# State-space heads of a hybrid block: the weighting, the inter-chunk output and the state update written with other instructions on other engines

## The chip, the cores and the metric

One core of a Trainium2 chip runs the whole kernel. The metric is the device time of one execution in microseconds; lower is better. The engines are TensorE (PE), VectorE (DVE), ScalarE (ACT), GpSimd (POOL) and SyncE (SP, which issues DMAs). Each takes its instructions from a queue of its own, in order.

## The reference

Two layers of a diffusion transformer block over 512 latent and 256 context tokens of 1024 features. Each layer projects the normalized tokens once and gives the columns to three kinds of heads: 6 of softmax attention, 4 of retention, 6 of a bidirectional state-space recurrence (SSD); an output projection and a squared-ReLU MLP follow. The recurrence in chunks of 128 tokens, cut to what matters here:

```python
scores = jnp.einsum('bhcin,bhcjn->bhcij', qc, kc) * decay
y_intra = jnp.einsum('bhcij,bhcjp->bhcip', scores, vc)
d_state = jnp.einsum('bhcj,bhcjn,bhcjp->bhcnp', jnp.exp(last - cum), kc, vc)
chunk_decay = jnp.exp(last[..., 0])
def step(s, inp):
    dec, ds = inp
    return dec[..., None, None] * s + ds, s
...
y_inter = jnp.exp(cum)[..., None] * jnp.einsum('bhcin,bhcnp->bhcip', qc, s_in)
return (y_intra + y_inter).reshape(b, h, l, p), s_final
```

It is run once forward and once backward; the keys of each direction are weighted by that direction's step size (dt), and the two outputs are added.

## The kernel before

Weights come from HBM and are split into a high and a low part, so that each product is three matmuls (`mm3`). Tokens lie in 6 tiles of 128: four latent, two context. In layer 0 the queries of all tiles are wanted (NQ = 6), in layer 1 only the latent ones (NQ = 4).

The state-space stage of a layer runs at about 148 to 262 us (layer 0) and 1219 to 1312 us (layer 1). Its loop goes over the heads h = 0 to 5 and mixes three things into each turn.

*Filling matmuls.* `run(fill, 1)` issues one tile of the query projection (24 matmuls `qap`), later of the gate z (`zp`). For each qap tile ACT copies the result out, POOL multiplies the gain (L570) and rotates it (L554 to L557).

*Inside a chunk* (`ssd_head_a`, `ssd_head_b`). Two matmuls broadcast the cumulative decays over the partitions (F, L747 and L749); ACT (L752), DVE (L754) and ACT again make the decay matrix `a`. The weighted scores `tb` join two triangles of `gfb` (the products of C and B, masked), one scaled by the forward step size, the other by the backward one: POOL writes the second for all tiles (L757), DVE adds the first, tile by tile, as scalar_tensor_tensor, STT (L759), and POOL multiplies by `a` (L760). PE then multiplies tb by the inputs (`yi`, L769), and DVE adds the result to `y_tok` (L771).

*Between chunks* (`ssd_state(i)`, one step of both directions). DVE weights the inputs (`vw`, L784). From the second step on PE multiplies the state `S` by C (`in`, L788), and DVE scales the result by the decay `expf` of the token and adds it to y_tok, head by head (L792). PE makes the step's state (`ds`, L797), and DVE scales S by the chunk's decay and adds ds, head by head (L803).

Behind the loop POOL multiplies y_tok by the gate (L869), ACT sums the squares and DVE makes the root from `ssq` (L871). Then attention starts: scores `s` (L938), the row maximum on DVE (L940, L943), probabilities `P` (L944, L949) and their transposes `pt`. The maximum needs `qrs`, the root of the queries' sums of squares, in three iterations of L165 to L167.

The program states dependences only: a scheduler fixes each engine's order when the kernel is built, within the limits of the pools. The matmul results `yi`, `in` and `ds` share one PSUM pool (pC) of two buffers, taken in turn; `s1` (vw, rotation scratch) has 3 buffers, `t3` (a, tb) 4, `u3` 6.

Of the kernel before, what the change touches and what calls it, by code (L numbers as in the profile page):

```python
# [14 lines left out]
AF = mybir.ActivationFunctionType  # L15
ALU = mybir.AluOpType
AX = mybir.AxisListType
PSUM = bass.MemoryType.PSUM
DRAM = bass.MemoryType.DRAM

D = 1024
# [13 lines left out]
# columns of w_in  # L35
QA, KA, VA, QR, KR, VR, GR, Z0, XBC, DT0 = 0, 384, 512, 640, 896, 1152, 1408, 1664, 2048, 2944
# rows of the per-layer parameters that are used as columns
R_B, R_G, R_CW, R_CB, R_SG, R_END = 0, 48, 80, 115, 122, 125
# columns of the per-layer parameters that are used on every partition
# [3 lines left out]
def shape_constants():  # L43
# [16 lines left out]
    # query minus key in a chunk; steps from the chunk before to a query, for both directions  # L60
# [20 lines left out]
def tile_hybrid_backbone(  # L81
# [87 lines left out]
    def rsqrt_mean(y, ssum, use, D=D, n=1):  # L169
        """1 / sqrt(ssum / D + EPS): the scalar engine's root, then one Newton step on its reciprocal"""  # L170
# [12 lines left out]
    def softplus(y, xin, n):  # L183
        """log(1 + exp(x)) = max(x, 0) + 2 atanh(e / (2 + e)), e = exp(-|x|)"""
# [17 lines left out]
    def wraw(src, shape, name):  # L202
        """one half of a unit: at most 1024 elements a partition"""
# [6 lines left out]
    def wunit(src, shape, name, lo_eng=None, pool=None):  # L210
        """src: function (first row block, row blocks) -> list of (AP, first column, columns)"""
# [13 lines left out]
    def wcols(w, k0, cols):  # L225
        """row blocks from k0 on; cols: list of (column in w, column in the unit, columns)"""
        return lambda a0, an: [(krows(w, k0 + a0, an, c, n), o, n) for c, o, n in cols]
# [21 lines left out]
    # gate * norm gain: [mixer or channel, stream]  # L249
    grow = [dp.tile([2, 2, D], F32, name=f"grow{l}") for l in range(DEPTH)]  # L250
    pcol = [cp.tile([128, R_END], F32, name=f"pcol{l}") for l in range(DEPTH)]
    # per layer: A1, B1, A2, B2, each [chunk, stream]
# [18 lines left out]
    def mod_cols(l, sec, q, nrow):  # L271
        """section of 512 columns of the modulation, as per-feature columns; q: [nrow, 512] in SBUF"""
# [75 lines left out]
    def mod_sums(l, sec, acc, raw=None):  # L348
        """the same, with the sums over the chunks off the tensor engine; acc [128, 2, 512]"""
# [22 lines left out]
    def cond_cols(n):  # L372
        """silu of both conditionings: [partition, chunk of 128 / n features, stream], the same on n groups of partitions"""
# [15 lines left out]
    def mod_groups(secs, acc, cs):  # L389
        """sections [(layer, section)] side by side on groups of partitions; acc [128, 2, 512]"""  # L390
# [27 lines left out]
    def gate_row(pool, l, which, stream):  # L418
        """(gate * norm_g) of one stream on every partition; which 0: mixer, 1: channel"""
# [1054 lines left out]
```

## Time and profile before

| | |
|---|---|
| runs (three) | 1886.2, 1888.09 (median), 1888.5 us |
| span of the profiled execution | 1880.8 us |
| busy: PE, DVE, ACT, POOL | 93%, 65%, 37%, 20% |
| mean granted TensorE clock | 0.972 |
| bytes moved | 217 MB, 115 GB/s over the span |

A run's time is taken around the whole launch, the span runs from the first to the last instruction of the one execution that was profiled; the median lies 7.3 us above it. The shares of busy time are averages over stages that differ, so the stage that is changed has to be read by itself, from the waits of the engine that is busiest in it.

### The profile page before, as it was taken

How to read it: one execution, taken by the hardware profiler on the slowest of the kernel's cores; microseconds unless marked ns; L12 is line 12 of the kernel's file. 1: busy time of each engine (PE TensorE's matmuls, PEld its weight loads, DVE VectorE, ACT ScalarE, POOL GpSimd, SP SyncE). 2: the span in 40 equal slices, each digit the busy share in tenths (PEclk: the TensorE clock that was granted, in tenths of full speed). 3: DMA queues.
4: the chain of work that ended last, by engine and by line, in shares of the span. 5: the costliest groups of instructions: out<-in, count | busy, mean ns of one | idle time of the engine just before them, and what ended most of it. 6: DMA issues, size and time to landing. Idle time of an engine off the chain costs nothing. (4 is left out here: it accounts for less than half of the span.)

```text
span 1880.8 us, 24641 instructions
## 1 busy us (share of the span) xinstructions
PE 1753.1 (93%) x8991; PEld 1443.0 (77%) x8991; DVE 1219.7 (65%) x2462; ACT 703.0 (37%) x1267; POOL 369.1 (20%) x391
## 2 busy tenths in 40 slices
PE   6987999997999999999999979888987999999998
PEld 2877977655878888888888868777866788888886
DVE  5868985664668566566566586788876654444445
ACT  5543376652461111201201275433772532222222
POOL 0047232313001100100100132553022021111112
PEclk9999999997999999999999999999996999999999
DMA  8410243366444334434434433224324432222332
GB/s 274 124 52 32 89 149 104 104 182 184 146 135 136 124 101 132 125 107 123 126 105 118 152 123 91 65 71 124 100 73 110 147 122 90 90 90 91 102 105 95
DMA packets 189078, 217.00 MB, mean 115 GB/s; under 512 B 67667, under 2 KB 142237, under 8 KB 188957
## 3 DMA queue, kind: packets, MB, share of 16 engines
q1 hardware_dynamic: 188956, 215.43, 37.8%
q8 instruction: 71, 1.16, 0.2%
q14 instruction: 51, 0.41, 0.1%
HBM read 189.66 MB, written 25.72 MB: 115 GB/s over the span
## 5 line engine op out<-in xcount | busy, mean ns | idle before, releaser
L467 PE MATMUL f<-h_h,wh_f 128*128 128x512 f32 (+1 forms) x800 | 280.3, 351 | 1.4 <-ACT h_h L448 1.4
L469 PE MATMUL f<-h_h,wl_f 128*128 128x512 f32 (+1 forms) x800 | 281.0, 352 | 0.0
L468 PE MATMUL f<-h_l,wh_f 128*128 128x512 f32 (+1 forms) x800 | 280.1, 350 | 0.8 <-DVE h_l L449 0.8
L1299 POOL TENSOR_TENSOR r<-r 128x768 f32<-128x768 f32 (+1 forms) x64 | 93.8, 1466 | 847.4 <-ACT r L1298 837.8
L467 PE MATMUL f<-wh_g,uh 128*128 128x512 f32 x640 | 253.0, 396 | 4.1 <-DVE acc L1327 1.7
L468 PE MATMUL f<-wl_g,uh 128*128 128x512 f32 x640 | 252.6, 395 | 0.0
L469 PE MATMUL f<-wh_g,ul 128*128 128x512 f32 x640 | 251.8, 394 | 0.0
L221 ACT ACTIVATE wh_f<-wr_f 128x1024 fp32r<-128x1024 f32 x64 | 66.5, 1055 | 377.2 <-PE f L469 164.4
L1329 DVE TENSOR_TENSOR acc<-acc,f 128x512 f32<-128x512 f32 x140 | 96.0, 686 | 121.0 <-PE f L469 119.6
L467 PEld LDWEIGHTS f<-h_h,wh_f 128*128 128x128 f32 x800 | 152.0, 190 | 23.0 <-ACT h_h L448 1.5
L468 PEld LDWEIGHTS f<-h_l,wh_f 128*128 128x128 f32 x800 | 151.1, 189 | 22.8 <-DVE h_l L449 1.0
L469 PEld LDWEIGHTS f<-h_h,wl_f 128*128 128x128 f32 x800 | 151.2, 189 | 20.8
L405 DVE SCALAR_TENSOR_TENSOR ga<-wr_mg,cg_a,ga 128x512 f32<-128x512 f32 x216 | 153.6, 762 | 14.6 <-DMA wr_mg<-in_w_mod_dram 14.6
L467 PEld LDWEIGHTS f<-wh_g,uh 128*128 128x128 f32 x640 | 120.1, 188 | 33.5 <-DVE acc L1327 2.2
L469 PEld LDWEIGHTS f<-wh_g,ul 128*128 128x128 f32 x640 | 120.1, 188 | 28.8
L468 PEld LDWEIGHTS f<-wl_g,uh 128*128 128x128 f32 x640 | 120.2, 188 | 27.4 <-DVE wl_g L222 0.2
L1298 ACT ACTIVATE r<-f 128x768 f32<-128x768 f32 (+1 forms) x64 | 44.8, 699 | 193.4 <-PE f L469 133.4
L1300 DVE CAST uh<-r 128x768 fp32r<-128x768 f32 (+1 forms) x64 | 32.3, 505 | 123.2 <-POOL r L1299 123.2
L222 DVE TENSOR_TENSOR wl_f<-wr_f,wh_f 128x1024 fp32r<-128x1024 f32 x64 | 77.6, 1220 | 51.3 <-ACT wh_f L221 51.3
L222 DVE TENSOR_TENSOR wl_g<-wr_g,wh_g 128x1024 fp32r<-128x1024 f32 x62 | 76.6, 1241 | 50.9 <-ACT wh_g L221 50.8
L221 ACT ACTIVATE wh_g<-wr_g 128x1024 fp32r<-128x1024 f32 x64 | 67.3, 1056 | 94.2 <-DMA wr_g<-in_w_ff_dram 53.6
L467 PE MATMUL xbc<-h_h,wh_xbc 128*128 128x512 f32 (+1 forms) x208 | 73.5, 353 | 7.7 <-ACT cin L692 7.7
(405 smaller groups left out, 3774.3 us busy)
## 6 DMA issues: line engine op xcount, KB each, us to landing
wr_f<-in_w_ff_dram SPq DMA_DIRECT2D x64, 512.0 KB, 3.7
wr_g<-in_w_ff_dram SPq DMA_DIRECT2D x64, 512.0 KB, 3.5
wr_mg<-in_w_mod_dram SPq DMA_DIRECT2D x192, 128.0 KB, 2.9
wr_m<-in_w_mod_dram SPq DMA_DIRECT2D x24, 512.0 KB, 3.8
m<-in_w_mod_dram SPq DMA_DIRECT2D x32, 256.0 KB, 4.2
wr_o<-in_w_out_dram SPq DMA_DIRECT2D x16, 512.0 KB, 4.1
wr_xbc<-in_w_in_dram SPq DMA_DIRECT2D x14, 512.0 KB, 5.3
xmid<-xt SPq DMA_DIRECT2D x10, 512.0 KB, 2.6
```

The lines of the kernel that those rows point to most:

```text
L221: S.activation(hv[:, a0 : a0 + an], r, AF.Copy)
L222: (lo_eng or V).tensor_tensor(lv[:, a0 : a0 + an], r, hv[:, a0 : a0 + an].bitcast(F32), ALU.subtract)
L405: V.scalar_tensor_tensor(acc[:, s], r2[:, k % 2], w, acc[:, s], ALU.mult, ALU.add)
L467: T.matmul(o, a[0], b[0], start=first, stop=False)
L468: T.matmul(o, a[0], b[1], start=False, stop=False)
L469: T.matmul(o, a[1], b[0], start=False, stop=last)
L1298: S.activation(r, q[:, :NT], AF.Relu)
L1299: G.tensor_tensor(r, r, r, ALU.mult)
L1300: V.tensor_copy(uh, r)
L1329: V.tensor_tensor(acc[tt][:, ns], acc[tt][:, ns], qs[tt][half], ALU.add)
```

## The change

Three places, all in the state-space stage. The weighted scores: POOL writes its triangle into a tile of its own, `tw` (pool u3); ACT writes the scaled other triangle into tb, tile by tile; one DVE addition joins them. The inter-chunk output: one DVE multiplication over all six heads writes `ys` (pool s1), and POOL adds it to y_tok. The state: POOL scales S for all six heads, and one DVE addition adds ds. Comments and docstrings are gone as well, so lines behind the first place are numbered one, later two and then one higher; the new lines are L758 (tw), L760 (ACT), L761 (DVE), L762 (POOL, tb by a), L794 (ys), L795 (POOL, y_tok), L804 (POOL, S), L805 (DVE, S), and vw is L786, in L790, ds L799, yi L771.

```diff
             tb = t3([128, 6, 128], f"tb{h}")
-            G.tensor_tensor(tb[:, :NQ], gf[:, 1, :NQ], bc(dtv[:, :NQ, 6 + h], 2, 128), ALU.mult)
+            tw = u3([128, 6, 128], f"tw{h}")
+            G.tensor_tensor(tw[:, :NQ], gf[:, 1, :NQ], bc(dtv[:, :NQ, 6 + h], 2, 128), ALU.mult)
             for t in range(NQ):
-                V.scalar_tensor_tensor(tb[:, t, :], gf[:, 0, t, :], dtv[:, t, h : h + 1], tb[:, t, :], ALU.mult, ALU.add)
+                S.activation(tb[:, t, :], gf[:, 0, t, :], AF.Copy, scale=dtv[:, t, h : h + 1])
+            V.tensor_tensor(tb[:, :NQ], tb[:, :NQ], tw[:, :NQ], ALU.add)
             G.tensor_tensor(tb[:, :NQ], tb[:, :NQ], a[:, :NQ], ALU.mult)
             mats[h] = tb
...
                     yv = v3(y_tok[:, t])
-                    for h in range(6):
-                        V.scalar_tensor_tensor(yv[:, h, :], q[:, h, :], expf[:, t, 6 * d + h : 6 * d + h + 1], yv[:, h, :],
-                                               ALU.mult, ALU.add)
+                    ys = s1([128, 6, 64], "ys")
+                    V.tensor_tensor(ys, q, bc(expf[:, t, hs], 2, 64), ALU.mult)
+                    G.tensor_tensor(yv, yv, ys, ALU.add)
...
                     if i == 0:
                         S.activation(st, q, AF.Copy)
                     else:
-                        for h in range(6):
-                            V.scalar_tensor_tensor(st[:, h, :], st[:, h, :], dec[:, t, 6 * d + h : 6 * d + h + 1], q[:, h, :],
-                                                   ALU.mult, ALU.add)
+                        G.tensor_tensor(st, st, bc(dec[:, t, hs], 2, 64), ALU.mult)
+                        V.tensor_tensor(st, st, q, ALU.add)
```

The scheduler's orders differ at many places; three of them follow. The first is POOL's queue in layer 0, from the first triangle of tb to the second tb product. Before (a number behind a name tells buffers apart: tb_1371 and tw_1372 are head 0's, tb_1467 or tb_1469 head 1's, st_qa_1566 or st_qa_1570 the query tile 2):

```order
L757 TENSOR_TENSOR tb_1371<-gfb_1348,dtv_664 128x768
L757 TENSOR_TENSOR tb_1467<-gfb_1348,dtv_664 128x768
L760 TENSOR_TENSOR tb_1371<-tb_1371,a_1351 128x768
L570 TENSOR_TENSOR st_qa_1566<-st_qa_1566,par_479 128x384
L554 TENSOR_TENSOR rp_1572<-st_qa_1566,cst_486 128x12x16
L555 TENSOR_TENSOR rp_1572<-st_qa_1566,cst_486 128x12x16
L556 TENSOR_TENSOR st_qa_1566<-st_qa_1566,cst_486 128x384
L557 TENSOR_TENSOR st_qa_1566<-st_qa_1566,rp_1572 128x384
L757 TENSOR_TENSOR tb_1598<-gfb_1348,dtv_664 128x768
L760 TENSOR_TENSOR tb_1467<-tb_1467,a_1447 128x768
```

After:

```order
L758 TENSOR_TENSOR tw_1372<-gfb_1348,dtv_664 128x768
L758 TENSOR_TENSOR tw_1470<-gfb_1348,dtv_664 128x768
L758 TENSOR_TENSOR tw_1603<-gfb_1348,dtv_664 128x768
L762 TENSOR_TENSOR tb_1371<-tb_1371,a_1351 128x768
L758 TENSOR_TENSOR tw_1739<-gfb_1389,dtv_664 128x768
L570 TENSOR_TENSOR st_qa_1570<-st_qa_1570,par_479 128x384
L554 TENSOR_TENSOR rp_1576<-st_qa_1570,cst_486 128x12x16
L555 TENSOR_TENSOR rp_1576<-st_qa_1570,cst_486 128x12x16
L556 TENSOR_TENSOR st_qa_1570<-st_qa_1570,cst_486 128x384
L758 TENSOR_TENSOR tw_1889<-gfb_1389,dtv_664 128x768
L762 TENSOR_TENSOR tb_1469<-tb_1469,a_1449 128x768
```

Three tw stand ahead of the first tb product instead of two first halves of tb, and two more between it and the second one. The queue goes on after that with the state of both directions (S_1336 forward, S_1337 backward) and the next query tile:

```order
L557 TENSOR_TENSOR st_qa_1570<-st_qa_1570,rp_1576 128x384
L804 TENSOR_TENSOR S_1336<-S_1336,dec_668 128x384
L570 TENSOR_TENSOR st_qa_1638<-st_qa_1638,par_479 128x384
L554 TENSOR_TENSOR rp_1644<-st_qa_1638,cst_486 128x12x16
L555 TENSOR_TENSOR rp_1644<-st_qa_1638,cst_486 128x12x16
L762 TENSOR_TENSOR tb_1602<-tb_1602,a_1582 128x768
L556 TENSOR_TENSOR st_qa_1638<-st_qa_1638,cst_486 128x384
L758 TENSOR_TENSOR tw_2018<-gfb_1389,dtv_664 128x768
L557 TENSOR_TENSOR st_qa_1638<-st_qa_1638,rp_1644 128x384
L795 TENSOR_TENSOR y_tok_1335<-y_tok_1335,ys_1655 128x384
L804 TENSOR_TENSOR S_1337<-S_1337,dec_668 128x384
L795 TENSOR_TENSOR y_tok_1335<-y_tok_1335,ys_1668 128x384
```

The backward state's L804 stands behind a rotation, head 2's tb product, a tw and a y_tok addition; before, POOL had nothing to do with S.

The second place is PE's queue in layer 0, in the second step (i = 1) and up to head 1's yi. Before, from the backward `in` on:

```order
L788 MATMUL in_1666<-S_1337,CT_978 128x192
L788 MATMUL in_1666<-S_1337,CT_1098 128x192
L749 MATMUL F_1736<-frow_671,onehot 128x256
L467 MATMUL qap_1755<-wh_qa_1390,h_h 128x384
L468 MATMUL qap_1755<-wl_qa_1391,h_h 128x384
L469 MATMUL qap_1755<-wh_qa_1390,h_l 128x384
L467 MATMUL qap_1755<-wh_qa_1390,h_h 128x384
L468 MATMUL qap_1755<-wl_qa_1391,h_h 128x384
L469 MATMUL qap_1755<-wh_qa_1390,h_l 128x384
L467 MATMUL qap_1755<-wh_qa_1390,h_h 128x384
L797 MATMUL ds_1675<-vw_1664,b_tok_673 128x192 x2
```

After, from the same `in` (in_1665) to yi of head 1 (yi_1676 and yi_1682, where yi_1684 was before):

```order
L790 MATMUL in_1665<-S_1337,CT_978 128x192
L790 MATMUL in_1665<-S_1337,CT_1098 128x192
L469 MATMUL qap_1686<-wh_qa_1392,h_l 128x384
L467 MATMUL qap_1686<-wh_qa_1402,h_h 128x384
L468 MATMUL qap_1686<-wl_qa_1403,h_h 128x384
L469 MATMUL qap_1686<-wh_qa_1402,h_l 128x384
L799 MATMUL ds_1671<-vw_1663,b_tok_673 128x192 x2
L771 MATMUL yi_1676<-xs_tok_672,tb_1469 128x128 x4
L771 MATMUL yi_1682<-xs_tok_672,tb_1469 128x128 x2
L467 MATMUL qap_1686<-wh_qa_1402,h_h 128x384
L468 MATMUL qap_1686<-wl_qa_1403,h_h 128x384
L469 MATMUL qap_1686<-wh_qa_1402,h_l 128x384
```

In the new order the two yi stand behind four qap matmuls and ds; before, twelve qap matmuls and ds lay between `in` and the first yi (the last five of the twelve are not shown), and four more between the two.

The third place is DVE's queue in layer 1, where the roots qrs are made. Before, its last iterations, among the start of attention:

```order
L165 TENSOR_TENSOR rq_t<-qrs_10548 128x36
L900 TENSOR_TENSOR qla_11350<-dTqa_11344,qha_11349 128x512
L166 TENSOR_TENSOR rq_t<-rq_t,rq_h 128x36
L940 TENSOR_REDUCE mx_11354<-s_11357 128x1
L167 SCALAR_TENSOR_TENSOR qrs_10548<-rq_t,qrs_10548 128x36
L940 TENSOR_REDUCE mx_11354<-s_11380 128x1
L165 TENSOR_TENSOR rq_t<-qrs_10548 128x36
L222 TENSOR_TENSOR wl_qg_12080<-wr_qg_0_12081,wh_qg_12079 128x1024
L871 TENSOR_SCALAR ssq_11216<-ssq_11216 128x6
L166 TENSOR_TENSOR rq_t<-rq_t,rq_h 128x36
L222 TENSOR_TENSOR wl_qg_12080<-wr_qg_2_12086,wh_qg_12079 128x1024
L158 TENSOR_SCALAR rq_t<-ssq_11216 128x6
```

After, right behind the fourth head's first instructions, where tb_10860 is head 3's:

```order
L159 TENSOR_SCALAR qrs_10498<-rq_t 128x36
L842 SCALAR_TENSOR_TENSOR st_zt_10840<-st_zt_10840,zh_10841 128x384
L754 SCALAR_TENSOR_TENSOR a_10846<-F_10853,ncol_9893,a_10846 128x128 x4
L165 TENSOR_TENSOR rq_t<-qrs_10498 128x36
L166 TENSOR_TENSOR rq_t<-rq_t,rq_h 128x36
L167 SCALAR_TENSOR_TENSOR qrs_10498<-rq_t,qrs_10498 128x36
L761 TENSOR_TENSOR tb_10860<-tb_10860,tw_10861 128x512
L165 TENSOR_TENSOR rq_t<-qrs_10498 128x36
L166 TENSOR_TENSOR rq_t<-rq_t,rq_h 128x36
L167 SCALAR_TENSOR_TENSOR qrs_10498<-rq_t,qrs_10498 128x36
L165 TENSOR_TENSOR rq_t<-qrs_10498 128x36
L166 TENSOR_TENSOR rq_t<-rq_t,rq_h 128x36
```

All three iterations stand ahead of the third step's vw now, and wl_qg's two halves (L222) stand in the fifth step, ahead of L941. In front of the first row maximum stands ssq instead:

```order
L910 TENSOR_TENSOR vat_11163<-vraw_11161,vat_11163 128x12x64
L893 SCALAR_TENSOR_TENSOR k1a_11232<-dTka_11225,k1a_11232 64x768
L901 TENSOR_TENSOR qla_11244<-dTqa_11238,qha_11243 128x512
L901 TENSOR_TENSOR qla_11256<-dTqa_11250,qha_11255 128x512
L872 TENSOR_SCALAR ssq_11122<-ssq_11122 128x6
L941 TENSOR_REDUCE mx_11260<-s_11263 128x1
L158 TENSOR_SCALAR rq_t<-ssq_11122 128x6
L160 TENSOR_SCALAR rq_h<-ssq_11122 128x6
L944 TENSOR_TENSOR mx_11260<-mx_11260,qrs_10498 128x1
```

## Rows read from the trace of the kernel before

**Rows 1.** The page: busy time of each engine, share of the span, instructions.

```profile
PE 1753.1 (93%) x8991; PEld 1443.0 (77%) x8991; DVE 1219.7 (65%) x2462; ACT 703.0 (37%) x1267; POOL 369.1 (20%) x391
```

**Rows 2.** PE's waits in layer 0, 148 to 262 us: total, times, longest.

```profile
PE ds L797 <- DVE vw L784: 4.4, 2, 2.7
PE yi L769 <- POOL tb L760: 3.6, 1, 3.6
PE s L938 <- DVE rq_t L165: 1.7, 1, 1.7
PE in L788 <- DVE y_tok L771: 1.6, 1, 1.6
...
PE in L788 <- DVE y_tok L792: 1.1, 1, 1.1
```

**Rows 3.** PE's waits in layer 1, 1219 to 1315 us, same columns.

```profile
PE ds L797 <- DVE vw L784: 5.9, 4, 2.5
PE yi L769 <- POOL tb L760: 3.7, 1, 3.7
PE s L938 <- ACT P L944: 2.3, 1, 2.3
...
PE pt L152 <- DVE P L949: 1.1, 1, 1.1
PE s L938 <- DVE qla L900: 0.8, 1, 0.8
```

**Rows 4.** Windows of layer 0: us, busy of each engine, granted clock, DMA share, GB/s.

```profile
core 0: us, PE busy (x) PEld busy (x) DVE busy (x) ACT busy (x) POOL busy (x), PEclk, DMA share, GB/s
...
160.00:170.00 10.00, 6.99 (x35) 6.85 (x36) 10.00 (x20) 2.39 (x7) 7.80 (x8) 0.83 0.06 20
```

**Rows 5.** Windows of layer 1 where attention begins, same columns.

```profile
1300.00:1310.00 10.00, 6.67 (x27) 4.90 (x26) 9.68 (x24) 3.25 (x8) 8.78 (x12) 0.86 0.40 118
1310.00:1330.00 20.00, 20.00 (x110) 16.74 (x111) 14.03 (x33) 15.46 (x32) 2.35 (x4) 0.90 0.29 82
```

**Rows 6.** Lines 759, 792 and 803: duration ns min/median/max, first and last start, forms.

```profile
L759 DVE SCALAR_TENSOR_TENSOR tb<-gfb,dtv,tb x60: 332/342/1566, 158.1 to 1282.3; 128x128 f32<-128x128 f32 x60
...
L792 DVE SCALAR_TENSOR_TENSOR y_tok<-in,expf,y_tok x108: 265/273/285, 179.9 to 1293.6; 128x64 f32<-128x64 f32 x108
...
L803 DVE SCALAR_TENSOR_TENSOR S<-S,dec,ds x96: 264/275/282, 181.0 to 1289.0; 128x64 f32<-128x64 f32 x96
```

**Rows 7.** Prices: three lines as in rows 6, and ACT's timeline at 157 us.

```profile
L222 DVE TENSOR_TENSOR wl_z<-wr_z,wh_z x8: 948/958/1352, 137.3 to 1245.1; 128x768 fp32r<-128x768 f32 x8
...
L784 DVE TENSOR_TENSOR vw<-xs_tok,wst x20: 544/551/2014, 150.0 to 1285.8; 128x384 f32<-128x384 f32 x20
...
L570 POOL TENSOR_TENSOR st_qa<-st_qa,par x10: 991/1016/1310, 142.7 to 1243.5; 128x384 f32<-128x384 f32 x10
...
157.08 1.66 ACT L752 ACTIVATE a<-F,ncol 128x128 f32<-128x128 f32 x6 [0.37 <-PE F L749]
```

**Rows 8.** Timeline at 178 us: start, us, engine, line, operation; idle before, releaser.

```profile
177.98 1.97 DVE L784 TENSOR_TENSOR vw<-xs_tok,wst 128x384 f32<-128x384 f32 x1
...
177.74 1.80 POOL L760 TENSOR_TENSOR tb<-tb,a 128x768 f32<-128x768 f32 x1 [1.35 <-DVE tb L759]
```

**Rows 9.** POOL's timeline in layer 0.

```profile
156.60 2.92 POOL L757 TENSOR_TENSOR tb<-gfb,dtv 128x768 f32<-128x768 f32 x2
161.15 1.80 POOL L760 TENSOR_TENSOR tb<-tb,a 128x768 f32<-128x768 f32 x1 [1.63 <-DVE tb L759]
...
164.04 0.60 POOL L554 TENSOR_TENSOR rp<-st_qa,cst 128x192 f32<-128x192 f32 x1
...
166.36 1.01 POOL L557 TENSOR_TENSOR st_qa<-st_qa,rp 128x384 f32<-128x384 f32 x1
```

**Rows 10.** POOL's timeline in layer 1.

```profile
1226.44 2.05 POOL L757 TENSOR_TENSOR tb<-gfb,dtv 128x512 f32<-128x512 f32 x2
1229.59 1.26 POOL L760 TENSOR_TENSOR tb<-tb,a 128x512 f32<-128x512 f32 x1 [1.10 <-DVE tb L759]
```

## The prediction

> **What bounds the kernel now.** I began with the busy shares of the page [rows 1]: PE works 93% of the span, the other engines 65%, 37% and 20%. So the time changes only where PE stands still or runs slowly, and an instruction saved on DVE is worth nothing unless PE waits for it. The change lies in two short stretches, the state-space stages of the two layers, and the second view is what PE waits for there. In layer 0 [rows 2] the six longest stalls are 2.7 + 1.7 (the rest of the 4.4) for DVE's vw, 3.6 for POOL's tb, 1.6 and 1.1 for DVE's y_tok, and 1.7 for DVE's rq_t where attention begins: 12.4 us. In layer 1 [rows 3] they are 5.9 for vw in four pieces, 3.7 for tb, and 0.8, 2.3 and 1.1 at the start of attention: 13.8 us.
>
> The third view gives what a stall costs on top. In windows of 10 us the granted clock is 0.83 right behind the 3.6 us stall of layer 0 [rows 4], and the same in three other windows of the two stages: behind the 2.7 us stall (180 to 190), and in layer 1 behind 3.7 us (1230 to 1240) and 2.5 us (1240 to 1250). A mean of 0.83 between the levels 1.0 and 0.5 is 10 x 0.17 / 0.5 = 3.4 us at the lower one, half of it lost: 1.7 us. The windows behind the shorter stalls, 1.7 us and less, show 1.00, so I count 1.7 us for each stall of 2.5 us or more. The start of attention in layer 1 [rows 5] has 0.86 and then 0.90 over 20 us: 1.4 + 2.0 = 3.4 us. **Ledger before:** layer 0 12.4 + 2 x 1.7 = 15.8 us; layer 1 13.8 + 2 x 1.7 + 3.4 = 20.6 us.
>
> **What the change takes from DVE.** Medians are 342, 273 and 275 ns [rows 6]. Layer 0 has 36 + 60 + 48 of them: 12.3 + 16.4 + 13.2 = 41.9 us. Layer 1 has 24 + 48 + 48: 34.5 us. What comes instead: one tb addition a head (priced by the 128x768 subtraction of two SBUF tiles, 0.95 us [rows 7]; two thirds of it, 0.64, for layer 1's 512 columns) and, for each step and direction, one ys and (from the second step) one S addition at 0.55 us, the price of vw, which has the same 128x384 [rows 7]. Layer 0: 6 x 0.95 + 10 x 0.55 + 8 x 0.55 = 15.6 us; layer 1: 6 x 0.64 + 16 x 0.55 = 12.6. DVE is relieved of 26 and 22 us in stretches of about 110 and 95 us.
>
> **What it gives to the others.** ACT gets 36 and 24 scaled copies; six ACT passes of 128x128 take 1.66 us [rows 7], so 10 and 7 us, on an engine busy 37% overall; hidden, except that the tb addition waits for six of them (bounds 0, if ACT runs ahead, to 1.7 us, once a layer at the first head, beside POOL's tw, which takes as long). I take 0. POOL gets 10 + 8 and 8 + 8 operations at 1.02 us [rows 7]: 18 and 16 us. POOL is idle most of these stretches, so the amount is no matter; the order is. Its queue runs strictly as written, and the S multiplication and the y addition now stand in it behind rotations (3.3 us a tile) and tb products of later heads.
>
> POOL's 1.02 against DVE's 0.55 us for the same 128x384 is 1.8 times. The Trainium skill, GPSIMD Engine Reference, section 4.1, tells to keep two-input elementwise work on VectorE, which it puts about 2 times faster; the rows agree in size. By that rule alone the 34 moved operations would make the kernel slower; a sum by engine time would not, since POOL idles. The walk below decides between the two.
>
> **Two costs of sharing.** DVE's vw, median 551 ns, took 1.97 us at 177.98, while POOL's tb product ran from 177.74 to 179.54 [rows 8]: it ended with POOL's instruction, not after its own length. L792, which reads PSUM, has a maximum of 285 ns [rows 6] and never shows this. So ys and the S addition (PSUM inputs) are free of it, while the tb addition and vw have 34 more POOL instructions to meet. Bounds per meeting: 0 to 1.5 us (2.01 at the worst less 0.55 [rows 7]); ten meetings a layer on an engine now with 20 us of slack I price at nothing unless PE stands at that vw. The Trainium skill, SBUF — State Buffer, section "Who interferes with whom", says the same: a DVE instruction with two SBUF inputs and a GpSimd one that reads SBUF lock each other out for a whole instruction. This trace agrees.
>
> **The walk, layer 0.** *First tb.* POOL now has three tw (2.92 us for two [rows 9], so 4.4 for three, from 156.6 to 161.0) before the first tb product, which before started at 161.15 and took 1.8 [rows 9]. The tb addition meets the third tw, so it runs from 161.0 to 161.9; the product ends at 163.7, 0.8 later than before. PE also arrives earlier at the waiting yi, since three qap matmuls and a decay broadcast now stand behind it: stall 3.6 becomes about 5.7. *Second step.* vw stands behind less work, but behind a tb addition and a tb product of POOL that overlap it: 2.7 becomes about 3.1; the 1.6 us for y_tok goes. *The first S multiplication of the second direction* is the new place. The rotation of tile 2 can now start only when its last three qap are through PE and ACT, behind that yi: about 5 us after 163.7, an estimate, so 168.9. From there POOL is never idle: two rotations with their gains (2 x 4.3: the four instructions from 164.04 to 167.37 [rows 9] and 1.02), two tb products (3.6), two tw (2.9) and, at 1.02 each, S, y addition, S: 18.2 us, and the S product ends at 187.1 or, with a lock or two, 187.6. PE's yi of head 1 takes its PSUM buffers in turn, behind ys and the S addition; between them and yi the new order leaves 4 qap matmuls, where 12 stood. PE is there at about 183.3 and goes on after the S addition, 188.2: a stall of 4.9 us. *Later* the stalls of 1.7 and 1.1 go (DVE is not late any more). *Attention start* about 1.5 instead of 1.7. Sum 5.7 + 3.1 + 4.9 + 1.5 = 15.2, with three slow windows, 5.1: **20.3, against 15.8: 4.5 us lost.**
>
> **The walk, layer 1.** *First tb.* Three tw of 1.03 and two S multiplications of 1.02 stand before the tb product (POOL free at 1226.44 [rows 10]): 1226.4 + 3.1 + 2.0 = 1231.5, + 1.3 = 1232.8, against 1230.85; and PE arrives 0.8 earlier: 3.7 becomes about 6.5. *vw* no longer waits behind tb's STTs, and the S multiplication is long done: 5.9 becomes about 1.0. Here one yi tile, not two, hangs on each step (4 tokens), so PE's buffers do not tie it to POOL. *Attention start.* The root iterations for q and the weight splits that stood at the very end of DVE's queue now stand two heads earlier; the 4.2 us and their 3.4 of slow clock become about 1.0 us and nothing. Sum 6.5 + 1.0 + 1.0 + 1.7 (one window) = **10.2, against 20.6: 10.4 us won.**
>
> **Sum:** + 4.5 - 10.4 = -5.9 us. The profiled span of 1880.8 becomes 1874.9; the runs' median lies 7.3 above the span, so **1882.2 us**. No change is what lies within 0.2%, 3.8 us.
>
> **Rivals.**
> A (the forecast), chance 0.46: 1879 to 1886.
> B: POOL is not late in layer 0. For it: all moved work fits into its idle time (20% busy). Against it: the fixed queue. The 4.9 us stall and its 1.7 go, and layer 0 turns from +4.5 to -2.1: 1876; if the first tb is on time also, some 4 less, 1872. Chance 0.15.
> C: what the start of attention gives does not come. There DVE's ssq, which needs POOL's products of y_tok and z, now stands before the first row maximum, and these products stand behind the y additions on POOL: 2 x 1.02, then 4 products of some 1.1. Of the 7.6 us of layer 1 (4.2 + 3.4) nothing is left if DVE stands there about 3 us. Price +6.6: 1889. Chance 0.22.
> D, slower: POOL's queue holds PE in layer 1 also. It decides if an S multiplication there starts behind a rotation of 3 us that waits for a late qap: then a stall of 3 to 5 us with a slow window, 1.7, at one or two of the four steps, +5 to +13 on the forecast: 1888 to 1896, 1893 as its middle. For it: the same queue does it in layer 0. Against it: S multiplications of layer 1 stand early in the order. Chance 0.17. The Trainium skill's rule on elementwise work above is on this side; no page decides between D and A.
>
> **Numbers.** The likeliest is A, 1882.2. Below 1872 is half of B at the most (0.05), above 1893 half of D (0.08): the range is 1872 to 1893. Faster by over 3.8 us (below 1884.3) is four fifths of A, and B: 0.37 + 0.15 = 0.52. Within it: the rest of A (0.09), three fifths of C (0.13), and a little of D: 0.24. Slower: the rest: 0.24.
>
> **What would show it.** In the profile after: PE's yi of the first head waits 5 to 7 us in both layers, longer than before (if not, the tw order costs nothing); in layer 0 a new PE wait of 4 to 5 us for S or ys at the second head, with POOL's L804 ending near 187 (if POOL is in time, B); in layer 1 no wait over 1.5 us for vw and the granted clock 1.0 from 1240 to 1260 and behind 1300 (if it stays 0.86 to 0.90 there, C); a wait for S in layer 1 of over 2 us means D. DVE's busy time must fall by some 48 us and POOL's rise by some 34. The forecast is wrong most easily in the order of POOL's queue: where a row there is released 2 us earlier or later than I worked out, a stall crosses the length that costs a slow window.

## The result: 15 us slower, where 6 us faster was forecast

The changed kernel takes 1903.7 us (median of 4 runs, 1896.7 to 1909.3) against 1888.3 us before (4 runs, 1886.2 to 1890.5): ratio 1.0082, 95% interval 1.0056 to 1.0107. That is 15.4 us slower and outside the range of the prediction. Its profiled execution took 1904.2 us for a span of 1902.4, so 1.8 us lie around a span, in this and all later runs. The 7.3 us that the prediction put there were mostly something else: the profiled execution of before was one of its quick ones, with a granted clock of 0.972, where its 99 runs in the comparisons below have 0.963 to 0.974 and take 1881.7 to 1896.6 us. So the spans differ by 21.6 us, the medians by 15.4.

The page of the changed kernel, same row as [rows 1]:

```profile
span 1902.4 us, 24533 instructions
...
PE 1766.3 (93%) x8991; PEld 1450.8 (76%) x8991; DVE 1183.0 (62%) x2244; ACT 718.8 (38%) x1327; POOL 406.4 (21%) x425
```

The engine work moved as intended: DVE has 36.7 us less, POOL 37.3 and ACT 15.8 us more. PE, with the same 8991 matmuls, is busy 13.2 us longer, and its granted clock is lower (0.964, before 0.972); it idles 8.4 us longer (1902.4 - 1766.3 = 136.1, before 127.7). What it waits for in layer 0, 148 to 275 us, answers to [rows 2] (total, times, longest):

```profile
PE ds L799 <- DVE vw L786: 7.7, 4, 2.5
PE yi L771 <- POOL tb L762: 5.6, 1, 5.6
PE yi L771 <- DVE ys L794: 3.5, 1, 3.5
PE s L939 <- ACT P L945: 1.9, 1, 1.9
...
PE yi L771 <- DVE S L805: 1.3, 1, 1.3
```

In layer 1, 1205 to 1335 us, [rows 3]:

```profile
PE yi L771 <- POOL tb L762: 6.8, 1, 6.8
PE ds L799 <- DVE vw L786: 5.7, 5, 3.2
...
PE s L939 <- ACT P L945: 1.2, 1, 1.2
PE ds L799 <- DVE S L805: 0.9, 1, 0.9
PE pt L152 <- DVE P L950: 0.9, 1, 0.9
PE yi L771 <- DVE S L805: 0.7, 1, 0.7
```

The 10 us windows of the two stages where the clock is below 1, and the one behind the start of attention in layer 1, columns as in [rows 4]; they answer to [rows 4, 5]. The other windows of the stages are at 1.00:

```profile
160.00:170.00 10.00, 4.41 (x18) 4.17 (x18) 6.71 (x11) 2.41 (x9) 7.12 (x5) 0.74 0.00 0
170.00:180.00 10.00, 8.41 (x44) 7.95 (x43) 6.24 (x14) 6.50 (x18) 8.54 (x8) 0.92 0.00 0
180.00:190.00 10.00, 5.58 (x21) 5.18 (x22) 3.16 (x5) 0.00 (x0) 9.92 (x11) 0.76 0.11 39
190.00:200.00 10.00, 10.00 (x56) 9.81 (x55) 4.81 (x12) 6.27 (x19) 2.76 (x4) 0.90 0.06 22
260.00:270.00 10.00, 8.09 (x34) 6.14 (x33) 7.14 (x25) 6.92 (x15) 2.85 (x5) 0.83 0.32 108
1240.00:1250.00 10.00, 3.17 (x14) 2.76 (x13) 4.05 (x8) 2.17 (x8) 8.43 (x9) 0.67 0.05 20
1250.00:1260.00 10.00, 10.00 (x48) 9.81 (x48) 6.98 (x14) 7.50 (x17) 8.71 (x8) 0.82 0.02 7
...
1310.00:1330.00 20.00, 17.23 (x92) 13.62 (x91) 11.52 (x34) 13.02 (x30) 8.96 (x13) 1.00 0.23 66
```

A window of 10 us at clock c loses 10 x (1 - c), as in the prediction. With that, and with every row of the two views of waits (also the small ones left out above), the stages cost:

| | stalls, layer 0 | slow clock | stalls, layer 1 | slow clock | sum |
|---|---|---|---|---|---|
| before | 15.9 | 3.4 | 16.9 | 6.8 | 43.0 |
| after | 23.0 | 8.5 | 19.9 | 5.1 | 56.5 |

So 13.5 of the 21.6 us by which the two profiled spans differ are lost inside the two stages, 12.2 of them in layer 0. The other 8 us lie outside, and they are slow clock, not stalls: PE idles 8.4 us longer in all, where the stalls of the stages alone grew by 10.1, and of its 13.2 us of longer work the slow clock of the stages explains 3.4. Whether the change or the one execution lowered the clock there, no run shows.

**Where the new stalls come from.** DVE's timeline in the changed kernel (the bracket is the engine's idle time before the row and what ended it):

```profile
160.05 2.22 DVE L761 TENSOR_TENSOR tb<-tb,tw 128x768 f32<-128x768 f32 x1 [2.29 <-POOL tw L758]
...
179.61 1.17 DVE L786 TENSOR_TENSOR vw<-xs_tok,wst 128x384 f32<-128x384 f32 x1 [2.22 <-POOL st_qa L557]
...
188.32 0.56 DVE L794 TENSOR_TENSOR ys<-in,expf 128x384 f32<-128x384 f32 x1 [5.05 <-POOL st_qa L557]
190.06 0.56 DVE L805 TENSOR_TENSOR S<-S,ds 128x384 f32<-128x384 f32 x1 [1.18 <-POOL S L804]
...
198.65 0.96 DVE L761 TENSOR_TENSOR tb<-tb,tw 128x768 f32<-128x768 f32 x1 [2.12 <-ACT tb L760]
...
217.39 2.17 DVE L842 SCALAR_TENSOR_TENSOR st_zt<-st_zt,zh 128x384 f32<-128x384 f32 x1
...
230.53 0.96 DVE L761 TENSOR_TENSOR tb<-tb,tw 128x768 f32<-128x768 f32 x1 [1.91 <-ACT tb L760]
231.41 1.18 DVE L842 SCALAR_TENSOR_TENSOR st_zt<-st_zt,zh 128x384 f32<-128x384 f32 x1
232.52 2.15 DVE L786 TENSOR_TENSOR vw<-xs_tok,wst 128x384 f32<-128x384 f32 x1
...
1272.83 1.14 DVE L167 SCALAR_TENSOR_TENSOR qrs<-rq_t,qrs 128x36 f32<-128x36 f32 x1
...
1275.13 0.55 DVE L786 TENSOR_TENSOR vw<-xs_tok,wst 128x384 f32<-128x384 f32 x1
```

And POOL's:

```profile
158.53 5.08 POOL L758 TENSOR_TENSOR tw<-gfb,dtv 128x768 f32<-128x768 f32 x3
163.57 2.11 POOL L762 TENSOR_TENSOR tb<-tb,a 128x768 f32<-128x768 f32 x1
...
187.30 0.99 POOL L557 TENSOR_TENSOR st_qa<-st_qa,rp 128x384 f32<-128x384 f32 x1
188.24 1.00 POOL L795 TENSOR_TENSOR y_tok<-y_tok,ys 128x384 f32<-128x384 f32 x1
189.20 0.83 POOL L804 TENSOR_TENSOR S<-S,dec 128x384 f32<-128x384 f32 x1
...
216.35 2.79 POOL L762 TENSOR_TENSOR tb<-tb,a 128x768 f32<-128x768 f32 x1
...
232.15 2.11 POOL L762 TENSOR_TENSOR tb<-tb,a 128x768 f32<-128x768 f32 x1
```

DVE is idle far more than before (busy 83.0 of the 127 us from 148 to 275, before 109.3), and its vw is late all the same. It waits for POOL and ACT, at the head of a queue in which vw stands: for a tw (at the first tb of each layer only), for ACT's half of tb (198.65, 230.53), and at 179.6 and 188.3 for a buffer of s1, which a rotation's scratch holds until POOL's L557. And it is held up: the vw at 232.52 ends at 234.67, 0.41 us behind POOL's product that ran beside it, as vw did before [rows 8]. The gate's row at 217.39, which has a median of 0.56 us, is held in the same way, and the vw of 219.48 stands behind it. The median vw takes 0.84 us now, 0.55 before [rows 7], but all 20 together 18.1 us, 16.6 before: it matters where such a lock falls, more than how many there are. PE's four longest waits for vw are read from these rows: 2.5 us in layer 0 for the buffer at 179.6, 2.2 for the gate's row, 2.4 for ACT's half of tb and then the lock on vw itself, and 3.2 in layer 1 for the rows of the root chain ahead of 1275.13.

### The profile page after: what moved, and what is told of

It is laid out like the page before. It is cut to its first block, busy times and chain, and to the rows that moved or that the text cites. A ratio compares the mean times of both kernels' runs of the same rounds, so it can differ in the third digit from the quotient of the medians.

```text
span 1902.4 us, 24533 instructions
## 1 busy us (share of the span) xinstructions
PE 1766.3 (93%) x8991; PEld 1450.8 (76%) x8991; DVE 1183.0 (62%) x2244; ACT 718.8 (38%) x1327; POOL 406.4 (21%) x425
## 5 line engine op out<-in xcount | busy, mean ns | idle before, releaser
L405 DVE SCALAR_TENSOR_TENSOR ga<-wr_mg,cg_a,ga 128x512 f32<-128x512 f32 x216 | 153.6, 762 | 15.1 <-DMA wr_mg<-in_w_mod_dram 15.1
L222 DVE TENSOR_TENSOR wl_g<-wr_g,wh_g 128x1024 fp32r<-128x1024 f32 x62 | 76.6, 1241 | 51.9 <-ACT wh_g L221 51.7
L222 DVE TENSOR_TENSOR wl_f<-wr_f,wh_f 128x1024 fp32r<-128x1024 f32 x64 | 77.6, 1220 | 49.7 <-ACT wh_f L221 49.7
```

The source lines that it names most:

```text
L222: (lo_eng or V).tensor_tensor(lv[:, a0 : a0 + an], r, hv[:, a0 : a0 + an].bitcast(F32), ALU.subtract)
L405: V.scalar_tensor_tensor(acc[:, s], r2[:, k % 2], w, acc[:, s], ALU.mult, ALU.add)
```

## The experiments

Ratios are to the kernel before, run beside each on the same chip, with 95% intervals; the medians of before were 1889.8 to 1890.9 us (1888.3 for the whole change). A difference between two of these ratios is good to 0.2 to 0.4 points. "Stalls" are PE's in the profiled execution, layer 0 + layer 1, as in the table above; in the row of the whole with a fourth s1 buffer 5.7 us for ACT's `cin`, a tile of the projection ahead of the stage of layer 1, are left out, since in the other kernels that stall falls before 1205 us.

| kernel | ratio | interval | stalls |
|---|---|---|---|
| weights alone | 1.0020 | 1.0006 to 1.0034 | 18.3 + 21.2 |
| output alone, y addition on POOL | 0.9974 | 0.9961 to 0.9987 | 14.2 + 12.8 |
| output alone, y addition on DVE | 0.9999 | 0.9984 to 1.0014 | 17.1 + 15.8 |
| state alone, S product on POOL | 1.0045 | 1.0029 to 1.0062 | 18.2 + 18.4 |
| state alone, S product on DVE | 1.0002 | 0.9987 to 1.0018 | 15.1 + 17.2 |
| weights + output | 1.0027 | 1.0014 to 1.0040 | 20.7 + 15.4 |
| **whole change** | 1.0082 | 1.0056 to 1.0107 | 23.0 + 19.9 |
| whole, S product on DVE | 1.0034 | 1.0018 to 1.0049 | 22.1 + 19.8 |
| whole, fourth s1 buffer | 1.0113 | 1.0093 to 1.0132 | 28.4 + 21.4 |
| weights alone, tiles exchanged | 0.9943 | 0.9925 to 0.9960 | 13.7 + 14.1 |
| exchanged weights + output | 0.9936 | 0.9916 to 0.9956 | 14.5 + 12.9 |
| ... + fourth s1 buffer | 0.9958 | 0.9944 to 0.9972 | 14.0 + 14.8 |
| whole, tiles exchanged | 0.9991 | 0.9972 to 1.0010 | 17.2 + 14.6 |
| ... + fourth s1 buffer | 1.0054 | 1.0036 to 1.0071 | 18.5 + 19.3 |
| whole, exchanged, S product on DVE | 0.9994 | 0.9976 to 1.0011 | 17.1 + 17.1 |
| ... + fourth s1 buffer | 1.0005 | 0.9988 to 1.0022 | 16.8 + 16.1 |

Theories that the expectations weigh, some of them by a letter: the joining addition makes DVE wait for ACT (W, later A); POOL's queue holds PE through the y additions and the S products (P); the ring of s1 does (R); what POOL does too early, tw and the S products, makes tb and vw late (Q); the form of the state over six heads costs by itself (F); the parts are harmless alone and collide (I).

**One part at a time.** Each is its piece of the diff of the change on the kernel before. The weights alone:

```diff
+            tw = u3([128, 6, 128], f"tw{h}")
...
-                V.scalar_tensor_tensor(tb[:, t, :], gf[:, 0, t, :], dtv[:, t, h : h + 1], tb[:, t, :], ALU.mult, ALU.add)
+                S.activation(tb[:, t, :], gf[:, 0, t, :], AF.Copy, scale=dtv[:, t, h : h + 1])
+            V.tensor_tensor(tb[:, :NQ], tb[:, :NQ], tw[:, :NQ], ALU.add)
```

> Only the first part of the change: tw on POOL, six scaled copies on ACT, one joining addition on DVE. Theory W (the weights do it: the joining addition waits for ACT's copies and for POOL, everything behind it on DVE, vw above all, is late, and the first tb comes later): slower than before by 8 to 15 us, with PE waiting 5 to 7 us for the first tb of each layer and 2 to 3 us at several vw. Rival P (POOL's queue does it, through the y additions and the S products): within 4 us of before. Rival R (ys takes a third user into the ring of three s1 buffers): within 4 us of before, apart from the first tb, 2 to 4 us.

Measured: 1892.6 us (11 runs), +0.20%: the first tb waits as long as W has it (5.6 and 5.2 us), but the loss is the small one of P and R. The output alone:

```diff
-                        V.scalar_tensor_tensor(yv[:, h, :], q[:, h, :], expf[:, t, 6 * d + h : 6 * d + h + 1], yv[:, h, :],
...
+                    V.tensor_tensor(ys, q, bc(expf[:, t, hs], 2, 64), ALU.mult)
+                    G.tensor_tensor(yv, yv, ys, ALU.add)
```

> Only the second part: one multiplication over six heads into ys on DVE, the addition to y_tok on POOL. Theory W: within 4 us of before, or faster by up to 5 us, since DVE is relieved and nothing waits for ACT. Rival P and rival R: slower by 4 to 10 us, with DVE's ys or vw idle behind a rotation of POOL (L557), 2 to 5 us at a time.

Measured: 1885.2 us, -0.26%: the only part that gains. The state alone:

```diff
-                            V.scalar_tensor_tensor(st[:, h, :], st[:, h, :], dec[:, t, 6 * d + h : 6 * d + h + 1], q[:, h, :],
...
+                        G.tensor_tensor(st, st, bc(dec[:, t, hs], 2, 64), ALU.mult)
+                        V.tensor_tensor(st, st, q, ALU.add)
```

> Only the third part: S times dec on POOL, one addition on DVE. Theory W: within 4 us of before. Rival P: slower by 3 to 8 us, with PE's yi or ds waiting for S. Rival R: within 4 us.

Measured: 1898.6 us (6 runs), +0.45%, the costliest part, in size as P has it. But no wait of PE for S is in its profile; what it waits for longer is vw (13.8 us, before 10.3) and the first tb of layer 1. Weights and output together, without the state:

> Parts one and two together, without the state. Alone they gave +3.8 and -4.9 us. Theory Q with costs that add up: within 4 us of before, and the third part is what makes the whole 15 us slower. Rival I (the parts collide: ys, y additions and tw share POOL's queue and the ring s1): slower by 6 us or more, with PE waiting over 3 us for ys or S at the second head of layer 0.

Measured: 1893.9 us, +0.27%, between the two; PE waits 2.8 us for ys at that place. The parts alone sum to +0.39% and the whole is +0.82%, so they also hurt each other: weights and output should give -0.06% by their sum, and give +0.27%. The second difference is clear of the noise, the first (0.43) just so.

POOL's queue of the state alone, at the first tb product of layer 1, and the row of DVE between, show how a small piece on POOL costs PE time; the wait of PE's yi there is 5.1 us (3.7 in [rows 3]):

```profile
1240.52 0.83 POOL L802 TENSOR_TENSOR S<-S,dec 128x384 f32<-128x384 f32 x1
1241.31 1.05 POOL L757 TENSOR_TENSOR tb<-gfb,dtv 128x512 f32<-128x512 f32 x1
1242.31 0.83 POOL L802 TENSOR_TENSOR S<-S,dec 128x384 f32<-128x384 f32 x1
1243.10 1.10 POOL L757 TENSOR_TENSOR tb<-gfb,dtv 128x512 f32<-128x512 f32 x1
1245.04 1.26 POOL L760 TENSOR_TENSOR tb<-tb,a 128x512 f32<-128x512 f32 x1 [0.84 <-DVE tb L759]
...
1242.40 2.48 DVE L759 SCALAR_TENSOR_TENSOR tb<-gfb,dtv,tb 128x128 f32<-128x128 f32 x4 [3.71 <-POOL tb L757]
```

Two S products, whose result is wanted much later, stand ahead of the tb product that PE waits for. They reach it through DVE's additions (L759), for which the product stands idle at the end: these start behind the first triangle, so behind the first S product, and take 2.48 us beside POOL's work, 1.91 before.

**The S product and the y addition on DVE.** The state alone with its product on DVE, then the output alone with its addition on DVE, then the whole change with the S product on DVE:

```diff
-                        G.tensor_tensor(st, st, bc(dec[:, t, hs], 2, 64), ALU.mult)
+                        V.tensor_tensor(st, st, bc(dec[:, t, hs], 2, 64), ALU.mult)
...
-                    G.tensor_tensor(yv, yv, ys, ALU.add)
+                    V.tensor_tensor(yv, yv, ys, ALU.add)
```

> The third part alone, with the product S times dec on DVE (0.55 us) instead of POOL. The state part on POOL gave +8.6 us and stalls of 18.2 and 18.4 us in the two layers. Theory Q (what POOL does earlier makes tb and vw late: two S products ahead of layer 1's first tb product, and every POOL instruction that holds DVE's two-input instructions): back to within 4 us of before, first tb of layer 1 waited for 3.7 us again, not 5.1. Rival F (the form does it: two operations over six heads in place of six short ones, the state is ready later): slower by 4 us or more, as on POOL.

Measured: 1888.0 us, +0.02%; yi's wait in layer 1 is 3.7 us again, as Q has it.

> The second part alone with the y addition on DVE too (two operations of 0.55 us in place of six of 0.27; no work goes to POOL). On POOL the part gave -4.9 us. If the gain is DVE's relief of 1.1 us a step: half of the gain or none, within 3 us of before. If it is the shorter chain from in to the next PSUM buffer (ys frees the buffer in 0.55 us instead of 1.2): the same gain, 3 to 6 us.

Measured: 1888.8 us, -0.01%: the gain of the output part is gone, so the shorter chain was not its source.

> The whole change with only S times dec on DVE in place of POOL. Theory Q: the 6.8 us wait for layer 1's first tb becomes about 5 (two S products less ahead of it), the wait for S in layer 0 goes: 6 to 10 us faster than the changed kernel, that is as parts one and two together, 4 to 8 us slower than before. Rival F (the form of the state does it): as slow as the changed kernel, 13 us or more.

Measured: 1897.6 us, +0.34%: of the loss of the whole, 0.82%, the place of the S product explains about half (0.48, good to 0.3). So the same move, two-input elementwise work from DVE to POOL, costs 0.43% for S (0.45 - 0.02) and gains 0.25% for y_tok, at about the same price an instruction. The Trainium skill, GPSIMD Engine Reference, section 4.1, tells to keep such work on VectorE; for S these runs agree, for the y addition they do not. The waits give a reading of the difference, which no run isolates. The S products stand ahead of the first tb product, as shown, and in the whole change PE also waits 3.3 us for S itself; for the y additions PE waits nowhere, and DVE in two places (2.5 us in the output alone).

**The tiles exchanged.** In the change POOL writes its triangle into tw, from pool u3 with 6 buffers, and can run ahead; in this edit POOL writes tb, as before, and ACT the new tile. The instructions stay the same in kind and number:

```diff
-            G.tensor_tensor(tw[:, :NQ], gf[:, 1, :NQ], bc(dtv[:, :NQ, 6 + h], 2, 128), ALU.mult)
+            G.tensor_tensor(tb[:, :NQ], gf[:, 1, :NQ], bc(dtv[:, :NQ, 6 + h], 2, 128), ALU.mult)
             for t in range(NQ):
-                S.activation(tb[:, t, :], gf[:, 0, t, :], AF.Copy, scale=dtv[:, t, h : h + 1])
+                S.activation(tw[:, t, :], gf[:, 0, t, :], AF.Copy, scale=dtv[:, t, h : h + 1])
```

On the weights alone:

> The first part alone with the two tiles exchanged: POOL writes its triangle into tb as before, ACT the other into tw, DVE adds. POOL's queue is then that of before at the first tb (two first products, not three tw, ahead of tb's product). Theory Q: the first tb is waited for about 3.6 us in both layers (not 5.6 and 5.2), and the part's +3.8 us become 0 or a gain of up to 4. Rival A (ACT's copies ahead of the joining addition do it, by holding DVE's queue): still +2 to +5 us, with vw waited for as long as in the first part alone (3.6 us in layer 0).

Measured: 1877.7 us (10 runs), -0.57%, where the weights alone had +0.20%: a gain of some 11 us, where Q allowed for 4 at most. POOL's queue at the first tb product of layer 0, the weights alone first:

```profile
157.31 5.07 POOL L758 TENSOR_TENSOR tw<-gfb,dtv 128x768 f32<-128x768 f32 x3
162.34 2.12 POOL L762 TENSOR_TENSOR tb<-tb,a 128x768 f32<-128x768 f32 x1
```

and with the tiles exchanged:

```profile
157.16 2.92 POOL L758 TENSOR_TENSOR tb<-gfb,dtv 128x768 f32<-128x768 f32 x2
161.04 1.81 POOL L762 TENSOR_TENSOR tb<-tb,a 128x768 f32<-128x768 f32 x1 [0.96 <-ACT sq L567]
```

The third triangle no longer stands ahead of the product. PE's first stall is 3.8 instead of 5.6 us in layer 0 (for DVE's gfb, no longer for the product), and 3.1 instead of 5.2 in layer 1: 3.9 us of the 11.7 by which the stalls fall (39.5 to 27.8). Another 3.6 us are the longest wait for vw in the weights alone, which the exchanged kernel does not have at that place. There vw waits for a buffer that comes free behind L557, and POOL has a tw and a tb product (174.49 to 177.02) between the third and the last instruction of that rotation:

```profile
173.05 1.49 POOL L758 TENSOR_TENSOR tw<-gfb,dtv 128x768 f32<-128x768 f32 x1
...
176.99 0.98 POOL L557 TENSOR_TENSOR st_qa<-st_qa,rp 128x384 f32<-128x384 f32 x1
...
178.00 1.33 DVE L786 TENSOR_TENSOR vw<-xs_tok,wst 128x384 f32<-128x384 f32 x1 [2.19 <-POOL st_qa L557]
```

The rest is smaller waits for vw and at the start of attention, behind an order that differs everywhere.

The exchange does a second thing, which the expectations overlooked. It is now ACT that writes the tile with 6 buffers and can run ahead, so DVE's joining addition waits for ACT nowhere; with the tiles as in the change it waits 2.3 us in the weights alone, in three places, and 6.9 in the whole, in six. So the exchange is a test of POOL's run-ahead and of A at the same time. In the weights alone it can be little of A: of the 2.3 us the 1.0 ahead of the longest wait for vw is covered by the 2.19 for the buffer. In the whole 1.9 us stand right ahead of a long wait (230.53 above).

On the whole change, and on weights and output:

> The whole change with only the two tiles of the weights exchanged: POOL writes tb, ACT tw. In the first part alone the exchange was worth 14 us (from +3.8 to -10.7). Theory Q (POOL's three tw ahead of the first tb product, and their run-ahead, cost the weights' part): 10 to 16 us faster than the changed kernel, so between 3 us faster and 5 us slower than before; what is left is the state product on POOL. Rival I (the collision of ys, S and rotations on POOL is the cost of the whole): still slower than before by 8 us or more.

Measured: 1889.4 us, -0.09%, as Q has it. The exchange alone takes the whole loss away.

> The two parts that gained: weights with exchanged tiles (-10.7 us) and output with the addition on POOL (-4.9 us), the state as before. If they add up: 13 to 18 us faster than before (some 1874). Rival I (both use POOL's queue at the second head): within 4 us of the exchanged weights alone (-7 to -12), or worse.

Measured: 1878.9 us (8 runs), -0.64%. The output's 0.26 points bring 0.07 here; the noise does not tell the two apart. This and the exchanged weights alone, equal within their intervals, beat both kernels. The S product moved to DVE beside the exchange:

> The whole change with both edits: tiles exchanged and S times dec on DVE. Theory Q: as weights exchanged and output together, since the state on DVE was worth nothing by itself: 10 to 18 us faster than before. Rival I: slower than the exchanged weights alone, less than 8 us faster than before.

Measured: 1887.9 us, -0.06%: Q's 10 to 18 us did not come, and rival I was right here. Each of the two edits helps the whole change by itself (0.91 and 0.48 points), and together they help no more than the exchange alone (0.88).

**The ring of s1.** The 5.05 us before ys at 188.32 looked like a fault of the ring: vw, ys and the rotations' scratch share three buffers. A fourth (room for it comes from a small tile that two names share):

```diff
-        s1 = lambda shape, name, dt=F32: mp.tile(shape, dt, tag="s1", name=f"{name}{l}", bufs=3)
+        s1 = lambda shape, name, dt=F32: mp.tile(shape, dt, tag="s1", name=f"{name}{l}", bufs=4)
```

On the whole change:

> The whole change, but the ring s1 (vw, rotation scratch, ys, gate scratch) has four buffers instead of three; the 32 bytes that were missing come from lg and ng sharing a tile. Rival R: the 3.5 us wait of PE for ys in layer 0 and DVE's 5.0 us idle behind POOL's L557 are gone, and with them 4 to 8 us of the changed kernel's time (some 1897). Theory W: that one wait goes at most, 2 to 4 us, and the kernel stays slower than before by 8 us or more.

Measured: 1912.3 us (5 runs), +1.13%, no better than the change (the intervals overlap). The wait for ys is gone, and PE's yi waits 7.2 us at the same place. DVE's row there:

```profile
188.77 0.56 DVE L805 TENSOR_TENSOR S<-S,ds 128x384 f32<-128x384 f32 x1 [7.99 <-POOL S L804]
```

and POOL's queue ahead of it:

```profile
186.01 0.99 POOL L557 TENSOR_TENSOR st_qa<-st_qa,rp 128x384 f32<-128x384 f32 x1
186.96 0.99 POOL L795 TENSOR_TENSOR y_tok<-y_tok,ys 128x384 f32<-128x384 f32 x1
187.91 0.83 POOL L804 TENSOR_TENSOR S<-S,dec 128x384 f32<-128x384 f32 x1
```

The ring was the wait that came last by the profile, and POOL's queue stood right behind it. The same fourth buffer beside the exchange, on weights and output, on the whole with the S product on DVE, and on the whole:

> Exchanged weights and output with the y addition on POOL, state as before, ring s1 with four buffers. If the ring costs here (1.5 us wait for ys in layer 0, no slow clock behind it): 1 to 4 us faster than with three buffers (-12), so -13 to -16. If the wait only moves on to the next thing, POOL's y addition or the S update: -8 to -13, the same.

Measured: 1882.0 us (7 runs), -0.42%.

> Exchanged weights, output with the y addition on POOL, state in two operations on DVE, ring s1 with four buffers. With three buffers this was as before (-1 us). Ring theory: the 2.9 us wait of PE for ys, and the fall of its clock to 0.66 from 180 to 190 us, are gone, and 5 to 10 us with them. Rival (the state's form costs it: PE waits 0.5 us for S at eight places): within 3 us of before still.

Measured: 1892.1 us, +0.05%.

> The whole change, tiles exchanged, S product on POOL, ring s1 with four buffers. With three: as before (-1 us). Ring theory: 4 to 8 us faster than before. Rival (POOL's queue: what no longer waits for the ring waits for the S product behind a rotation, as the whole change with four buffers did, 7.2 us for S): 0 to 8 us slower than before.

Measured: 1901.2 us (5 runs), +0.54%; at the slow end of the rival's 0 to 8 us or beyond it; DVE waits 5.37 us for POOL's S product here. In no case does the buffer help, so the ring theory falls.

## Why the prediction was wrong

*Right: the first tb product.* Forecast 5.7 and 6.5 us, measured 5.6 and 6.8. Without the third tw ahead of it (tiles exchanged) PE no longer waits for the product in layer 0, but 3.8 us for gfb, and 3.1 us for it in layer 1; without the two S products the 6.8 are 5.3. In layer 0 the agreement is in part luck: the addition ended at 162.27, before the third tw and not behind it, while that tw took 2.2 us beside the addition, not 1.5.

*Right in place, its cause half right: the second head of layer 0.* Forecast a stall of 4.9 us for S behind POOL's queue, with L804 ending at 187.1 to 187.6. Measured 3.5 + 1.3 us, L804 ending at 190.03. Of the 5 us that DVE stood there first, the prediction knew nothing: ys needs an s1 buffer that the rotation holds until L557. With a fourth buffer POOL's S product is what is waited for.

*Wrong, the step that failed: "Later the stalls of 1.7 and 1.1 go (DVE is not late any more)", and "vw no longer waits behind tb's STTs": 5.9 would become 1.0.* Measured for vw: 7.7 us in layer 0, where 3.1 was forecast, and 5.7 in layer 1, with 1.6 more for S. The argument was that DVE, relieved of 26 and 22 us, would be early. Over the kernel it was relieved of 36.7 us, where these add up to 48: six short instructions in a row overlap (those of 0.27 us take 1.23 together), so the old ones kept DVE busy 69.6 us and not 76.4 (count times median), and the new ones 31.1 and not 28.2. But it did stand idle more, and vw came no earlier. By the waits it is the order, not the volume, that makes it late: in front of it now stand a tb addition that waits for ACT (6.9 us over the kernel), the wait for a buffer behind POOL's L557, locks beside POOL's 34 more instructions, and in layer 1 six rows of the root chain, which was put there from the end (at 1272.83 one of 0.2 us takes 1.14). I had priced ACT's share and the locks at nothing, because DVE had slack.

The root chain is also what became of the start of attention in layer 1, 4.2 us before. There it went as forecast in kind: 2.4 us, of which 2.1 for the probabilities, and the clock is 1.00 from 1310 to 1330 where it was 0.90 [rows 5]. Rival C is out. But the chain came back as the 3.2 us stall for vw.

*Too small: the slow clock.* I counted 1.7 us for each stall of 2.5 us or more: 5.1 and 1.7. Measured 8.5 and 5.1: 3.4 us behind the stall of 5.6 and 5.1 behind that of 6.8. The rule failed on both sides of its 2.5 us as well: the window 260 to 270, behind a stall of 1.9, lost 1.7, and the one behind the 3.2 us for vw in layer 1 is at 1.00.

Together: forecast 20.3 and 10.2 us for the two ledgers; with the same items (without xt, G, qap and DMA waits) they are 20.4 + 8.5 = 28.9 and 16.5 + 5.1 = 21.6. The sum, 50.5, is 14.1 above the ledger before (15.8 + 20.6; 12.7 with the small waits that it left out), where 5.9 below was forecast. Rival D, slower, had the side and its mechanism in part: POOL's queue does hold PE in layer 1, but at the first tb product; the waits for S there are 0.9 and 0.7 us, not 3 to 5.

*Shown by the runs:* which engine gets the new tile is worth 0.77 to 0.91 points (weights alone; whole), the whole of the loss, and the S product on POOL costs 0.43 to 0.48 (state alone; whole). The two savings overlap. Of the 11.7 us of stalls that the exchange saves in the weights alone, 7.5 can be pointed to in POOL's queue, as Q has it (3.9 at the first products, 3.6 at vw behind a tw and a product). W falls in the size that it gave itself (+0.20% for the weights alone); P holds for S in price, though not by waits for S in the state alone, and fails for the y additions; R fell; F is not seen in the state alone; of I there is a part, 0.43 points by which the whole costs more than its parts. *Not shown:* how much of the whole's loss is DVE's 6.9 us behind ACT (A), since the exchange takes these away too; and why the state over six heads, free by itself on DVE (+0.02%), costs 0.6 points beside exchanged weights and output (-0.64 to -0.06%). PE's waits for S there add up to 5.2 us, where the other has 1.5, and a fourth buffer leaves the distance (-0.42 to +0.05%). Each edit reorders all engines, so a cause inside one order is read from the waits, not isolated by a run.

## What to carry to other kernels

Relieving an engine that is 65% busy brought nothing by itself here: ask, for each instruction that PE waits for, what stands ahead of it in its queue after the change and which engines that waits for. Work put on a mostly idle in-order engine is not free if somebody soon waits for what stands behind it: the y addition gained there, the S product lost. And a new tile in a deep pool lets its producer run ahead, of more urgent instructions too; giving that tile to the other engine was worth about what the whole change had cost.

## What the runs showed of the hardware

Beside a product of POOL, DVE's vw ends at a fixed distance behind it: the vw of layer 0 (232.52 + 2.15 = 234.67) and, before, the one of [rows 8] (177.98 + 1.97 = 179.95) end 0.41 us behind the end of POOL's product (234.26 and 179.54), though one began 0.37 and the other 0.24 us behind its start. The other rows of vw and of the gate (L842, L841 before) that took over 0.6 us do the same: each ends 0.41 or 0.42 us behind the end of an instruction of POOL, 10 of 10 before and 13 of 13 in the changed kernel.

The low clock does not follow from the length of a stall alone. The whole change and the weights alone have the same first stall of 5.6 us; behind it the granted clock is 0.74 and 0.92 in two windows in the one, 0.83 and 1.00 in the other. Exchanged weights with output, and exchanged weights alone, both stand 3.8 us: 0.83 and 0.67 from 160 to 170. What decides it the runs don't show, so a price of one fixed loss for each stall, as the prediction had it, is good to a factor of two at best.
